# Linear attention with key-value matrices between the halves of the tokens, and splits of two heads at once, in a transformer block on one core

## The chip, the core and the metric

The kernel runs on one core of a Trainium2 chip. Its time is the device time of one execution in microseconds (us); the figure given for a kernel is the median of several runs. Every run is also described by a profile of one execution, with its own time. Engines are called as the profile calls them: PE (TensorE, matrix products; PEld are its weight loads), ACT (ScalarE), DVE (VectorE), POOL (GpSimd), SP (SyncE, which issues most DMAs).

## What is computed

One block of a transformer over 512 tokens of width 1024, in float32. The normed input is multiplied with one large matrix, and its columns are split into the inputs of two branches and their gates. The linear attention has 4 heads with keys of 128 and values of 256; the latent attention (MLA) has 8 heads, softmax over all 512 tokens, a key of 64 plain and 32 rotary features and a value of 128. Both outputs are gated, summed, projected, and followed by a squared-ReLU MLP.

The part that the change touches first is the linear attention. It is run once forwards and once backwards, and the results are added:

```python
def gla_direction(q, k, v, log_a, include_diag):
    ...
    b = jnp.cumsum(log_a, axis=3)
    q_dec = q * jnp.exp(b)
    k_dec = k * jnp.exp(-b)
    k_end = k * jnp.exp(b_last - b)
    scores = jnp.where(mask, jnp.einsum('bhnck,bhnsk->bhncs', q_dec, k_dec), 0.0)
    o_intra = jnp.einsum('bhncs,bhnsv->bhncv', scores, v)
    def step(state, inp):
        qc, kc, vc, dc = inp
        o = jnp.einsum('bhck,bhkv->bhcv', qc, state)
        state = state * dc[..., None] + jnp.einsum('bhck,bhcv->bhkv', kc, vc)
        return state, o
```

In words: a token's output is a sum over the earlier (or later) tokens of a decayed product of query and key, times the value. It can be had as scores times values, or, between two groups of tokens, by way of a matrix of keys times values (128x256) that the queries of the other group are multiplied with.

## The kernel before

**Split operands.** Most products take operands that are split into a high part of type fp32r and a low part, the rest. `mm3` (L87) makes three products of them: high x high, high x low, low x high (L88, L89, L90). `split` (L92) makes the two parts: ACT copies the high part (L93), DVE subtracts it from the source (L94). `split_scaled` (L96 to L98) does the same with a factor. A few small products take plain float32 operands, which PE works through in more than one pass; the profile counts such an instruction twice (x2).

**Linear attention.** The 512 tokens are 4 blocks of 128. For each head, class `Scaled` makes queries and keys times their decays: `near` within a block, `nxt` from a block to its neighbour in the same half of the tokens, `far` between the halves. `gla_scores` (L540) makes for each block j of keys a row of scores, in one PSUM bank (128x512): its own block (L555, and `bd` for the other direction, L543, copied under a mask by DVE, L570), its neighbour (L556) and the two blocks of the other half (L557, 256 columns). Each of the four rows is split by ACT (L571) and DVE (L566). `gla_out` (L717) multiplies: for each of 4 blocks of queries, 4 blocks of scores times 256 columns of values, `mm3` each, 48 products.

The heads stand in the loop at L1226 (heads 0 to 2), and head 3 behind it (L1273). Between a head's scores and its output PE runs a projection of 24 products (`proj_run`), and the other engines make the next head's gates: logarithms, running sums (`sums`), exponentials (`exps`, L478), `within` and `across`, whose products with broadcast factors run on POOL. In head 3 the projection is `zb5`. While it runs, ACT splits the normed latent queries (`cqhl`, L810) and makes the rotary tables (`tables`, L842: a table load, sine, cosine); DVE applies them to the rotary keys (`rotary_k`, L875: `krsin` and three more) and then makes the diagonal matrices `ckvdg` (L292) with the norms of the latent keys. Behind `gla_turn` and `gla_out` PE multiplies these with ones (`ckvrs`, L301), which spreads the norms over partitions, then runs the rotary queries (`ro`), the gates `zb6` and `zb7` and the first two heads' `uq`, `uk`, `uv`.

**Order.** In this part the order of PE, ACT, DVE and POOL is written out: `in_program_order` (L1308 to L1310) ties each instruction to the one before it in the text, for ACT and DVE from the start and for PE from the first large products up to `zb7`. SP's queue is ordered by the scheduler. All engines work strictly in the order of their queues.

**PSUM** has eight banks of 128x512, in two groups of four with the tags "at" and "mm"; a new accumulator waits until a bank of its group is released by its last reader.

**Latent attention.** `up_units` (L1007) prepares two heads at a time (a pair): it loads their weights, lets the rotary rows of the queries be copied from a shared tile by four DMAs (L1034), makes the plain rows of the queries for both heads in one accumulator (`uq`, partitions 0 to 63 the first head, 64 to 127 the second), splits each half into its own tile `q` (rows 0 to 63; the rotary rows are 64 to 95), does the same for the keys (`uk` into two of four tiles `kbuf`, whose rotary rows stay from one pair to the next), and makes the values (`uv`). Pair 0 is prepared ahead of the attention. The loop at L1330 has 32 steps n, one for each head and block of 128 queries: scores (L1064), softmax, transposes of the probabilities (L1091) and values (L1096); pair p is prepared in the steps before n = 8p, when its first head is due. In the loop the engines' orders are the scheduler's, with a few ties (`goes_behind`).

Of the kernel before, what the change touches and what calls it, by code (L numbers as in the profile page):

```python
# [13 lines left out]
I32 = mybir.dt.int32  # L14
AF = mybir.ActivationFunctionType
ALU = mybir.AluOpType
# [40 lines left out]
def tile_block(ctx: ExitStack, tc: tile.TileContext, t, out: bass.AP):  # L57
# [26 lines left out]
    def raw(x):  # L84
        return x.bitcast(F32)

    def mm3(acc, lh, ll, rh, rl, start, stop, onto=False):  # L87
        nc.tensor.matmul(acc, lh, rh, start=start, stop=False, skip_group_check=onto)  # L88
        nc.tensor.matmul(acc, lh, rl, start=False, stop=False, skip_group_check=onto)  # L89
        nc.tensor.matmul(acc, ll, rh, start=False, stop=stop, skip_group_check=onto)  # L90
# [447 lines left out]
            return self.near, self.nxt, self.far  # L538

    def gla_scores(near, nxt, far):  # L540
        bd = ps("at", "bd")
        for j in range(NT):
            nc.tensor.matmul(  # L543
                bd[:, j * P : (j + 1) * P], near["b"][:, 1, j], near["b"][:, 0, j], start=True, stop=True
            )
        bds = u2("bds")
        nc.scalar.activation(bds, bd, AF.Copy)  # L547
        res, scs = [], []
        for j in range(NT):
            sc = ps("at", f"sc{j}")  # L550
            dj = slice(j * P, (j + 1) * P)
            n = j + 1 if j % 2 == 0 else j - 1
            far_q = slice(2, 4) if j < 2 else slice(0, 2)
            far_c = slice(2 * P, 4 * P) if j < 2 else slice(0, 2 * P)
            nc.tensor.matmul(sc[:, dj], near["f"][:, 1, j], near["f"][:, 0, j], start=True, stop=True)  # L555
            nc.tensor.matmul(sc[:, n * P : (n + 1) * P], nxt[:, 1, j], nxt[:, 0, n], start=True, stop=True)  # L556
            nc.tensor.matmul(  # L557
                sc[:, far_c], far[:, 1, j], far[:, 0, far_q].rearrange("p a b -> p (a b)"),
                start=True, stop=True,
            )  # L560
            hl = u4(f"sc{j}")
            scs.append(sc)
            res.append(hl)

        def remainder(j):
            nc.vector.tensor_tensor(res[j][:, 1, :], scs[j], raw(res[j][:, 0, :]), op=ALU.subtract)  # L566

        for j, sc in enumerate(scs):
            dj = slice(j * P, (j + 1) * P)
            nc.vector.copy_predicated(sc[:, dj], after.bitcast(I32), bds[:, dj])  # L570
            nc.scalar.activation(res[j][:, 0, :], sc, AF.Copy)  # L571
            if j:
                remainder(j - 1)
        remainder(NT - 1)
        return res

# [137 lines left out]
        g = g1[i, half]  # L714
        nc.vector.scalar_tensor_tensor(g, dst, 1.0, g, op0=ALU.add, op1=ALU.mult)

    def gla_out(h, sc, rows=range(NT)):  # L717

        half, at = h // 2, (h % 2) * GDV
        accs = {j: ps("at", f"gla{h}o{j}") for j in sorted({i // 2 for i in rows})}  # L720
        c = slice(at, at + GDV)
        os = []
        for i in rows:
            o = accs[i // 2][:, (i % 2) * GDV : (i % 2 + 1) * GDV]
            tok = slice(i * P, (i + 1) * P)
            for j in range(NT):
                mm3(o, sc[j][:, 0, tok], sc[j][:, 1, tok], v[j, half][:, 0, c], v[j, half][:, 1, c],
                    j == 0, j == NT - 1)
            os.append(o)
        return os  # L730

    def gla_squares(h, os):
# [274 lines left out]
    def up_units(pr):  # L1007

        wq = stage(3, P, f"wq{pr}")
        for k in range(3):  # L1010
            nc.sync.dma_start(
                wq[:, k, :].rearrange("p (h e) -> p h e", h=2), w_uq[:, k, 2 * pr : 2 * pr + 2, 0:NOPE]
            )
        wqh, wql = halves(3, P, f"wq{pr}")
        split(wqh, wql, wq, nc.gpsimd)
        wk = stage(2, 384, f"wk{pr}")
        nc.sync.dma_start(
            wk.rearrange("p k (h e) -> p k h e", h=2), w_ukv[:, :, 2 * pr : 2 * pr + 2, :]
        )
        wh, wl = halves(2, 384, f"wk{pr}")  # L1020
        src = wk.rearrange("p k (h e) -> p k h e", h=2)
        for k in range(2):
            for c, e in ((slice(0, 128), slice(0, NOPE)), (slice(128, 384), slice(NOPE, 192))):
                split(wh[:, k, c].rearrange("p (h e) -> p h e", h=2),
                      wl[:, k, c].rearrange("p (h e) -> p h e", h=2), src[:, k, :, e], nc.gpsimd)
        if pr == 0:
            yield
        qs = []
        for i in range(2):
            q = u4(f"q{pr}{i}")  # L1030
            h = (2 * pr + i) * HALF
            for x in range(2):
                at = NOPE + x * HALF
                nc.sync.dma_start(raw(q[at : at + HALF]), raw(ro[x][h : h + HALF]))  # L1034
            qs.append(q)
        yield
        accq = up_T(wqh, wql, cq, f"uq{pr}")
        for i in range(2):
            split_scaled(qs[i][0:64, 0, :], qs[i][0:64, 1, :], accq[i * 64 : i * 64 + 64, :], QK_SCALE)
        yield  # L1040
        acck = up_T(wh[:, :, 0:128], wl[:, :, 0:128], ckv, f"uk{pr}")
        for i in range(2):
            kb = kbuf[2 * (pr % 2) + i]
            split(kb[0:64, 0, :], kb[0:64, 1, :], acck[i * 64 : i * 64 + 64, :])
        yield
        vs = []
        for j in range(2):
            acc = ps("mm", f"uv{pr}{j}")
            for i in range(2):
                tok = slice((2 * j + i) * P, (2 * j + i + 1) * P)  # L1050
                for k in range(2):
                    mm3(acc[:, i * 256 : i * 256 + 256], ckv[k][:, 0, tok], ckv[k][:, 1, tok],
                        wh[:, k, 128:384], wl[:, k, 128:384], k == 0, k == 1)
            hl = u4(f"v{pr}{j}", F32R, (P, 2, 2, 256))
            flat = [hl[:, x].rearrange("p a b -> p (a b)") for x in range(2)]
            split_scaled(*flat, acc, 0.5)
# [167 lines left out]
    rotary = Rotary()  # L1224
    pooled = traced()
    for h in range(GH - 1):  # L1226
        sc = gla_scores(*scaled_qk.parts())
        scaled_qk = Scaled(h + 1)
        gate = Gates(h + 1)
        gate.logs()  # L1230
        latent, j = ((cq_, 1), (cq_, 2), (ckv_, 0))[h]
        acc = latent.products(j)
        if h < 2:
            w_b, lows = begin_late(C_GQ + (h + 2) * P, f"gq{h + 2}")
        else:
            ckv_.begun[1], lows = begin_late(C_CKV + P, "ckv1")
        (rotary.angles, rotary.reduced, cq_.diagonals)[h]()
        gate.sums("f")
        gate.exps("f")
        lows()  # L1240
        latent.keep(j, acc)
        gate.sums("b")
        gate.exps("b")
        scaled_qk.within("f", gate.parts)
        scaled_qk.across("f", gate.parts)
        if j:
            latent.add_squares()
        if h:
            gla_turn(h - 1)
        os = gla_out(h, sc)  # L1250
        scaled_qk.within("b", gate.parts)
        rs = gla_squares(h, os)
        scaled_qk.across("b", gate.parts)
        if h < 2:
            w_k = begin_qk(h + 2, 1)
            gla_gated(h, os, rs)
            finish_qk(h + 2, 0, w_b)
            if h == 0:
                cq_.begin(2)
            else:  # L1260
                ckv_.begin(0)
                cq_.sums()
# [11 lines left out]
    sc = gla_scores(*scaled_qk.parts())  # L1274
    ckv_.sums()
    zb5 = proj_run(w_b, xT)
    cq = cq_.normed()
    cos, sin = rotary.tables()
    late = [over_rms(acc, f"b{f}") for f, acc in ((4, zb), (5, zb5))]
    rotary_k()  # L1280
# [6 lines left out]
    os = gla_out(h, sc)  # L1287
    rs = gla_squares(h, os)
    ckv_.spread()
    ckv = ckv_.normed()  # L1290
# [451 lines left out]
```

## Time and profile before

| | |
|---|---|
| runs before | 757.74, 757.77, 757.97 us; median 757.77 |
| the profiled execution | 757.43 us, of which the profile spans 755.7 |
| granted clock of PE in it | 0.999 of full speed |

| stretch, us | what runs | PE busy | DVE busy | ACT busy | POOL busy |
|---|---|---|---|---|---|
| 0 to 174.5 | first projections, large products by seven multiplications | 172.96 | 141.01 | 110.56 | 48.67 |
| 174.5 to 297.8 | linear attention, preparation of the latent attention | 123.30 | 95.51 | 79.88 | 52.40 |
| 297.8 to 377 | latent attention | 78.71 | 69.09 | 69.16 | 37.38 |
| 377 to 755 | output projection and MLP | 372.07 | 280.80 | 202.18 | 27.12 |

How to read the rows of the profile. A row of a timeline has start and duration in us, the engine, the line of the kernel, the operation, output<-inputs by name, their shapes, and how many instructions are merged in it; in brackets stands how long the engine sat idle before it and what ended that. A row of PE's waits has line and operand, who was waited for, and the us in total, the times and the longest. A row of DMA issues has the size of one and the median us from issue to landing. A matmul's duration is longer than its distance to the next, because matmuls are pipelined: the work of PE is read from the starts.

### The profile page before, as it was taken

The numbers are of one execution on the slowest core, as the hardware profiler recorded it, in microseconds if no ns is written. First come the engines' busy times: TensorE is split into PE (matmuls) and PEld (weight loads), VectorE is DVE, ScalarE is ACT, GpSimd is POOL, SyncE is SP. The second block draws the span as 40 slices with busy tenths as digits, with TensorE's granted clock in tenths as the row PEclk, the third lists the DMA queues.
The fourth block names the chain that finished last, engine by engine and source line by source line (L and its number), as shares of the span: only waits on it lengthen the run. The fifth ranks groups of instructions, "written<-read, shape, count | busy, mean of one in ns | idle before, by whom it ended". The sixth has DMA issues, their size and how long they took to land.

```text
span 755.7 us, 10257 instructions
## 1 busy us (share of the span) xinstructions
PE 747.1 (99%) x3720; PEld 632.7 (84%) x3720; DVE 586.4 (78%) x850; ACT 461.8 (61%) x780; POOL 165.6 (22%) x238
## 2 busy tenths in 40 slices
PE   9999999999999999999999999999999999999996
PEld 7888888888888888898888988888888888888885
DVE  7777886989787597898897787856696578748795
ACT  7556574686476575988865766345544555345644
POOL 0722110262662622136750100000000000000014
PEclk9999999999999999999999999999999999999999
DMA  9849582611321335228888421461126410650003
GB/s 312 259 117 240 173 175 82 113 29 29 83 55 31 49 81 119 74 84 201 260 161 262 134 57 55 141 193 57 56 63 204 123 57 2 203 158 0 29 1 111
DMA packets 94306, 87.59 MB, mean 116 GB/s; under 512 B 15696, under 2 KB 66896, under 8 KB 94256
## 3 DMA queue, kind: packets, MB, share of 16 engines
q1 hardware_dynamic: 87760, 74.33, 33.1%
q0 software_dynamic: 6208, 12.32, 9.2%
q8 instruction: 29, 0.48, 0.3%
q10 hardware_dynamic: 288, 0.28, 0.1%
q14 instruction: 21, 0.17, 0.1%
HBM read 83.25 MB, written 2.10 MB: 113 GB/s over the span
## 4 chain that ended last, share of the span: by engine, by line
PE 96%; ACT 1%; DVE 1%; issue 0%; POOL 0%; POOLq 0%; ACTq 0%
PE f L89 8%; PE f L90 8%; PE f L88 8%; PE gx L88 4%; PE gx L89 4%; PE gx L90 4%; PE first L330 3%; PE gz L89 2%; PE gz L90 2%; PE gz L88 2%; PE zb L88 1%; PE tp L1091 1%; PE zb L90 1%; PE zb L89 1%; PE wox L88 1%; PE wox L90 1%
## 5 line engine op out<-in xcount | busy, mean ns | idle before, releaser
L1681 POOL DMA_DIRECT2D gfin<-in_g_final x1 | 0.6, 628 | 283.8 <-PE f L90 283.8
L961 DVE TENSOR_TENSOR w<-w,w 128x1024 f32<-128x1024 f32 x32 | 38.7, 1220 | 0.3
L1071 DVE TENSOR_REDUCE top<-s 128x1 f32<-128x512 f32 x32 | 21.8, 681 | 3.8 <-PE s L90 3.5
L1076 ACT ACTIVATE e<-s,top 128x512 f32<-128x512 f32 x32 | 22.0, 688 | 2.9 <-DVE top L1071 2.7
L1419 DVE TENSOR_TENSOR h<-h,gx 128x512 f32<-128x512 f32 x32 | 21.5, 681 | 1.9 <-PE gx L90 1.8
L94 DVE TENSOR_TENSOR pT<-tp,pT 128x512 fp32r<-128x512 f32 x32 | 21.7, 681 | 1.5 <-ACT pT L93 1.3
L93 ACT ACTIVATE pT<-tp 128x512 fp32r<-128x512 f32 x32 | 19.0, 596 | 2.2 <-PE tp L1091 2.1
L1091 PE MATMUL tp<-ident,e 128*128 128x128 f32 x128 | 19.5, 274 | 0.3 <-ACT e L1082 0.2
L88 PE MATMUL av<-pT,v 128*128 128x256 f32 x64 | 19.1, 298 | 0.0
L93 ACT ACTIVATE ghb<-y 128x512 fp32r<-128x512 f32 x16 | 10.1, 632 | 14.0 <-DVE y L907 14.0
L1485 ACT ACTIVATE fa<-f 128x512 f32<-128x512 f32 x32 | 18.5, 578 | 0.0
L1091 PEld LDWEIGHTS tp<-ident,e 128*128 128x128 f32 x128 | 15.1, 140 | 4.0 <-ACT e L1082 1.0
L89 PE MATMUL av<-pT,v 128*128 128x256 f32 x64 | 18.2, 285 | 0.0
L90 PE MATMUL av<-pT,v 128*128 128x256 f32 x64 | 18.2, 284 | 0.0
L547 ACT ACTIVATE bds<-bd 128x512 f32<-128x512 f32 x4 | 2.4, 598 | 20.9 <-PE bd L543 20.9
L93 ACT ACTIVATE b_00h<-w 128x1024 fp32r<-128x1024 f32 x7 | 7.4, 1059 | 12.6 <-PE gz L90 6.0
L93 ACT ACTIVATE b_20h<-w 128x1024 fp32r<-128x1024 f32 x7 | 7.4, 1061 | 12.1 <-PE gx L90 6.0
L93 ACT ACTIVATE b_10h<-w 128x1024 fp32r<-128x1024 f32 x7 | 7.4, 1060 | 12.1 <-PE gx L90 6.0
L88 PE MATMUL s<-kbuf,q 96*128 96x512 f32 x32 | 14.2, 443 | 0.2 <-ACT e L1076 0.2
L1494 ACT ACTIVATE px<-fa 128x256 f32<-128x256 f32 x32 | 13.4, 418 | 1.0
L957 POOL DMA_DIRECT2D w<-in_w_out x10 | 12.3, 1403 | 7.6 <-DVE bo60l L94 6.5
L636 POOL DMA_DIRECT2D gvw<-in_w_in x4 | 4.8, 1227 | 38.7 <-DVE gvw L641 34.0
(1731 smaller groups left out, 2947.6 us busy)
## 6 DMA issues: line engine op xcount, KB each, us to landing
w<-in_w_ff SPq DMA_DIRECT2D x64, 256.0 KB, 3.4
w<-in_w_out POOLq DMA_DIRECT2D x10, 512.0 KB, 9.3
grw<-in_w_in SPq DMA_DIRECT2D x8, 512.0 KB, 9.0
zaw<-in_w_in SPq DMA_DIRECT2D x8, 512.0 KB, 7.0
gvw<-in_w_in SPq DMA_DIRECT2D x8, 512.0 KB, 4.5
w<-in_w_out SPq DMA_DIRECT2D x16, 256.0 KB, 6.2
x<-in_xt SPq DMA_DIRECT2D x8, 256.0 KB, 5.3
vw<-in_w_first SPq DMA_DIRECT2D x8, 256.0 KB, 5.5
```

The costliest lines, as they stand in the source:

```text
L88: nc.tensor.matmul(acc, lh, rh, start=start, stop=False, skip_group_check=onto)
L89: nc.tensor.matmul(acc, lh, rl, start=False, stop=False, skip_group_check=onto)
L90: nc.tensor.matmul(acc, ll, rh, start=False, stop=stop, skip_group_check=onto)
L93: nc.scalar.activation(hi, src, AF.Copy)
L94: rest.tensor_tensor(lo, src, raw(hi), op=ALU.subtract)
L330: nc.tensor.matmul(f_accs[i], a[:, i * P : (i + 1) * P], b, start=k == 0 and x == 0, stop=k == KD - 1 and x == 2)
L961: nc.vector.tensor_tensor(wq[dst][g], wq[x][g], wq[y][g], op=op)
L1071: nc.vector.tensor_reduce(top, acc, axis=AX.X, op=ALU.max, negate=True)
L1076: nc.scalar.activation(e, acc, AF.Exp, bias=top, accum_out=tot[:, qt % 2 : qt % 2 + 1])
L1091: nc.tensor.transpose(tp[:, k * P : (k + 1) * P], e[:, k * P : (k + 1) * P], ident)
L1419: nc.vector.tensor_tensor(hc, hc, acc, op=op)
L1485: nc.scalar.activation(a, acc, AF.Relu)
```

## The change

It has two parts.

**Linear attention.** The score rows shrink to the blocks within a half: two banks (`sc0`, `sc1`) with 2x2 blocks each, in place of four rows. PE transposes the four blocks of `far` keys into a bank `kt` (tokens on partitions), which ACT and DVE split (`keys`). A new function `gla_state` multiplies these with the values, 12 products, into one matrix of 128x256 for each half of the tokens; ACT copies them into SBUF (`state`). In `gla_out` each block of queries takes 2 blocks of scores (24 products for the head), and then one float32 product of its `far` queries with the other half's matrix. `gla_state` stands behind the projection and the running sums in the loop, ahead of `gate.exps("f")`; in head 3 it stands behind `cq_.normed()` and ahead of `rotary.tables()`.

**Splits of two heads.** For the pairs 1 and 2 (heads 2 to 5), the accumulators of queries and keys are split as a whole, 128 partitions at once, into the first head's tile. A DMA then copies rows 64 to 127 to rows 0 to 63 of the second head's tile. The first head's rotary rows of the queries, which the split writes over, are copied in behind that by two DMAs; the rotary rows of the first key tile are restored from the second by another. Pairs 0 and 3 stay as they are.

```diff
     def gla_scores(near, nxt, far):
...
+        scs = [ps("at", f"sc{g}") for g in range(2)]
+        def block(j, i):
+            at = (j % 2) * 256 + (i % 2) * P
+            return scs[j // 2][:, at : at + P]
+        for j in range(NT):
+            n = j + 1 if j % 2 == 0 else j - 1
+            nc.tensor.matmul(block(j, j), near["f"][:, 1, j], near["f"][:, 0, j], start=True, stop=True)
+            nc.tensor.matmul(block(j, n), nxt[:, 1, j], nxt[:, 0, n], start=True, stop=True)
+        kt = ps("at", "kt")
+        for j in range(NT):
+            nc.tensor.transpose(kt[:, j * P : (j + 1) * P], far[:, 1, j], ident)
         bds = u2("bds")
         nc.scalar.activation(bds, bd, AF.Copy)
+        res = [u4(f"sc{g}") for g in range(2)]
+        for g in range(2):
+            for j in (2 * g, 2 * g + 1):
+                nc.vector.copy_predicated(block(j, j), after.bitcast(I32), bds[:, j * P : (j + 1) * P])
+            nc.scalar.activation(res[g][:, 0, :], scs[g], AF.Copy)
+        for g in range(2):
+            nc.vector.tensor_tensor(res[g][:, 1, :], scs[g], raw(res[g][:, 0, :]), op=ALU.subtract)
+        keys = u4("kT")
+        split(keys[:, 0, :], keys[:, 1, :], kt)
+        return res, keys, far
+
+    def gla_state(h, keys):
+        half, at = h // 2, (h % 2) * GDV
+        c = slice(at, at + GDV)
+        acc = ps("at", f"gla{h}st")
         for j in range(NT):
...
+            tok = slice(j * P, (j + 1) * P)
+            mm3(acc[:, (j // 2) * GDV : (j // 2 + 1) * GDV], keys[:, 0, tok], keys[:, 1, tok],
+                v[j, half][:, 0, c], v[j, half][:, 1, c], j % 2 == 0, j % 2 == 1)
+        state = u2(f"gla{h}s")
+        nc.scalar.activation(state, acc, AF.Copy)
+        return state
...
-    def gla_out(h, sc, rows=range(NT)):
+    def gla_out(h, sc, state, far):
...
+        for i, o in enumerate(os):
+            g = i // 2
+            for x in range(2):
+                j = 2 * g + x
+                tok = slice(x * 256 + (i % 2) * P, x * 256 + (i % 2 + 1) * P)
+                mm3(o, sc[g][:, 0, tok], sc[g][:, 1, tok], v[j, half][:, 0, c], v[j, half][:, 1, c],
+                    i % 2 == 0 and x == 0, False, True)
+        for i, o in enumerate(os):
+            other = 1 - i // 2
+            nc.tensor.matmul(
+                o, far[:, 0, i], state[:, other * GDV : (other + 1) * GDV], start=False, stop=True,
+                skip_group_check=True,
+            )
...
+        apart = pr in (0, MH // 2 - 1)
+        qs = [u4(f"q{pr}{i}") for i in range(2)]
+        for i in range(2):
+            if apart or i == 1:
+                rotary_rows(i)
         yield
         accq = up_T(wqh, wql, cq, f"uq{pr}")
...
+            split_scaled(qs[0][:, 0, :], qs[0][:, 1, :], accq, QK_SCALE)
+            nc.sync.dma_start(raw(qs[1][0:64]), raw(qs[0][64:128]))
+            rotary_rows(0)
         yield
         acck = up_T(wh[:, :, 0:128], wl[:, :, 0:128], ckv, f"uk{pr}")
...
+            split(kbs[0][:, 0, :], kbs[0][:, 1, :], acck)
+            nc.sync.dma_start(raw(kbs[1][0:64]), raw(kbs[0][64:128]))
+            nc.sync.dma_start(raw(kbs[0][64:96]), raw(kbs[1][64:96]))
...
     for h in range(GH - 1):
-        sc = gla_scores(*scaled_qk.parts())
+        sc, keys, far = gla_scores(*scaled_qk.parts())
...
         gate.sums("f")
+        state = gla_state(h, keys)
         gate.exps("f")
...
     h = GH - 1
...
     cq = cq_.normed()
+    state = gla_state(h, keys)
     cos, sin = rotary.tables()
```

More of the change, by code (lines that the diff above doesn't have):

```diff
@@ L546, in gla_scores @@
         bds = u2("bds")
         nc.scalar.activation(bds, bd, AF.Copy)
-        res, scs = [], []
-        for j in range(NT):
[L550 to L575, printed above, removed]
+        res = [u4(f"sc{g}") for g in range(2)]
@@ L715, in za_rows @@
         nc.vector.scalar_tensor_tensor(g, dst, 1.0, g, op0=ALU.add, op1=ALU.mult)
-    def gla_out(h, sc, rows=range(NT)):
+    def gla_out(h, sc, state, far):
         half, at = h // 2, (h % 2) * GDV
-        accs = {j: ps("at", f"gla{h}o{j}") for j in sorted({i // 2 for i in rows})}
+        accs = [ps("at", f"gla{h}o{g}") for g in range(2)]
         c = slice(at, at + GDV)
[L722 to L729, printed above, removed]
+        os = [accs[i // 2][:, (i % 2) * GDV : (i % 2 + 1) * GDV] for i in range(NT)]
+        for i, o in enumerate(os):
[11 more added lines that the diff above has]
+            )
         return os
@@ L1027, in up_units, with rotary_rows @@
             yield
-        qs = []
-        for i in range(2):
-            q = u4(f"q{pr}{i}")
+        def rotary_rows(i):
             h = (2 * pr + i) * HALF
@@ L1033, in up_units @@
                 at = NOPE + x * HALF
-                nc.sync.dma_start(raw(q[at : at + HALF]), raw(ro[x][h : h + HALF]))
-            qs.append(q)
+                nc.sync.dma_start(raw(qs[i][at : at + HALF]), raw(ro[x][h : h + HALF]))
+        apart = pr in (0, MH // 2 - 1)
[3 more added lines that the diff above has]
+                rotary_rows(i)
         yield
         accq = up_T(wqh, wql, cq, f"uq{pr}")
-        for i in range(2):
-            split_scaled(qs[i][0:64, 0, :], qs[i][0:64, 1, :], accq[i * 64 : i * 64 + 64, :], QK_SCALE)
+        if apart:
+            for i in range(2):
+                split_scaled(qs[i][0:64, 0, :], qs[i][0:64, 1, :], accq[i * 64 : i * 64 + 64, :], QK_SCALE)
+        else:
+            split_scaled(qs[0][:, 0, :], qs[0][:, 1, :], accq, QK_SCALE)
+            nc.sync.dma_start(raw(qs[1][0:64]), raw(qs[0][64:128]))
+            rotary_rows(0)
         yield
         acck = up_T(wh[:, :, 0:128], wl[:, :, 0:128], ckv, f"uk{pr}")
-        for i in range(2):
-            kb = kbuf[2 * (pr % 2) + i]
-            split(kb[0:64, 0, :], kb[0:64, 1, :], acck[i * 64 : i * 64 + 64, :])
+        kbs = kbuf[2 * (pr % 2) : 2 * (pr % 2) + 2]
+        if apart:
+            for i, kb in enumerate(kbs):
+                split(kb[0:64, 0, :], kb[0:64, 1, :], acck[i * 64 : i * 64 + 64, :])
+        else:
+            split(kbs[0][:, 0, :], kbs[0][:, 1, :], acck)
+            nc.sync.dma_start(raw(kbs[1][0:64]), raw(kbs[0][64:128]))
+            nc.sync.dma_start(raw(kbs[0][64:96]), raw(kbs[1][64:96]))
         yield
@@ L1249, in tile_block @@
             gla_turn(h - 1)
-        os = gla_out(h, sc)
+        os = gla_out(h, sc, state, far)
         scaled_qk.within("b", gate.parts)
@@ L1273, in tile_block @@
     h = GH - 1
-    sc = gla_scores(*scaled_qk.parts())
+    sc, keys, far = gla_scores(*scaled_qk.parts())
     ckv_.sums()
@@ L1286, in tile_block @@
     gla_turn(h - 1)
-    os = gla_out(h, sc)
+    os = gla_out(h, sc, state, far)
     rs = gla_squares(h, os)
```

## The prediction

> **What bounds the kernel now.** I read the page first (busy shares, the chain that ended last), then PE's waits, then the timelines of PE, ScalarE and VectorE around the change.
>
> ```profile
> span 755.7 us, 10257 instructions
> PE 747.1 (99%) x3720; PEld 632.7 (84%) x3720; DVE 586.4 (78%) x850; ACT 461.8 (61%) x780; POOL 165.6 (22%) x238
> ...
> PE 96%; ACT 1%; DVE 1%; issue 0%; POOL 0%; POOLq 0%; ACTq 0%
> ```
>
> ```profile
> PE warm L320 <- POOL ident masks.py:199: 1.5, 1, 1.5
> PE tp L1091 <- ACT e L1082: 0.2, 1, 0.2
> PE s L88 <- ACT e L1076: 0.2, 1, 0.2
> ```
>
> TensorE is busy from end to end. Its three named waits come to 1.9 us, of which 1.5 is the start. So a matmul that goes shortens the run by its full pitch (start to start), a matmul that comes lengthens it likewise, and a new wait of PE costs its whole length. The other engines matter only where they make PE late. The busy time of a group is no price, since matmuls overlap; I take pitches.
>
> **The linear attention, one head.** Head 0 on PE, scores and then output:
>
> ```profile
> 174.55 1.05 PE L543 MATMUL bd<-qkb 128*128 128x128 f32 x8
> 175.44 0.39 PE L555 MATMUL sc<-qkf 128*128 128x128 f32 x2
> 175.66 0.39 PE L556 MATMUL sc<-qk 128*128 128x128 f32 x2
> 175.89 0.60 PE L557 MATMUL sc<-qk 128*128 128x256 f32 x2
> 176.32 0.38 PE L555 MATMUL sc<-qkf 128*128 128x128 f32 x2
> ...
> 179.19 0.40 PE L451 MATMUL gateb<-z,gate_b 128*128 128x512 f32 x1
> ...
> 184.86 0.28 PE L88 MATMUL gla0o<-gv,sc 128*128 128x256 f32 x1
> ...
> 190.62 0.40 PE L88 MATMUL gq<-xT,gq2h 128*128 128x512 f32 x1
> ```
>
> The trace before has transposes of the form that is added (four of 128x128 into one bank), in the attention; first their group on the page, then four of them with what follows:
>
> ```profile
> L1091 PE MATMUL tp<-ident,e 128*128 128x128 f32 x128 | 19.5, 274 | 0.3 <-ACT e L1082 0.2
> ```
>
> ```profile
> 327.71 0.60 PE L1091 MATMUL tp<-ident,e 128*128 128x128 f32 x4
> 328.07 0.47 PE L88 MATMUL s<-kbuf,q 96*128 96x512 f32 x1
> 328.38 0.40 PE L89 MATMUL s<-kbuf,q 96*128 96x512 f32 x1
> 328.62 0.40 PE L90 MATMUL s<-kbuf,q 96*128 96x512 f32 x1
> ```
>
> Prices: a float32 product of 128 columns 0.22 us (175.44 to 175.66), of 256 columns 0.43 (175.89 to 176.32), a product of 256 columns from split operands 0.12 (48 of them from 184.86 to 190.62). Four transposes hold PE 0.36 us, and the product behind them takes 0.31 where the next takes 0.24: 0.44 together.
>
> 1. Scores. Before, bd to gate b takes 4.64 us (174.55 to 179.19). After: bd 0.89, eight products of 128 columns 1.78, four transposes with their tail 0.44, gate f 0.23, together 3.34: **-1.30**. The four far products (1.72) are gone, the transposes have come.
> 2. Key-value matrices. New: 4 blocks x 3 products = 12 x 0.12 = **+1.44**.
> 3. Output. Before, 48 products, 184.86 to 190.62, 5.76 us. After: 24 x 0.12 = 2.88, and four float32 products of 256 columns with the state, of the very form of L557, 4 x 0.43 = 1.72; together 4.60: **-1.16**.
>
> Net -1.02 us a head: half the output products go, and half of that returns as key-value products. Four heads: -4.1 us, if PE waits for nothing.
>
> ScalarE and VectorE in the scores: four score copies become two plus the keys' split, and VectorE loses one subtraction; the keys have the time of a projection, 24 products of 512 columns at 0.23 or 5.5 us, to get ready before PE asks. New on ScalarE is the state's copy, 0.6 us (an activation of this shape, the sine below, takes 0.63). It waits for the last key-value product, and everything later on ScalarE stands behind it, since ScalarE's and VectorE's order here is that of the program. In heads 0 to 2 that is the reload of the exponential table and the exponentials. They then start about when they do now on the head's own clock, while PE is 1 us ahead. On VectorE a second scan and a difference (L468, L473) still stand before their first use, and they hide it: I cost it at nothing; uncovered, it would be that 1 us per head.
>
> **Head 3 is different.** There the sine table stands behind the copy:
>
> ```profile
> 265.79 1.83 ACT L810 ACTIVATE cqhl<-cqc 128x512 fp32r<-128x512 f32 x3 [1.62 <-DVE cqc L808]
> 267.63 1.28 ACT L844 ACT_TABLE_LOAD   x1
> 268.93 0.63 ACT L844 ACTIVATE sin<-ang 128x512 f32<-128x512 f32 x1
> ```
>
> ```profile
> 270.36 0.48 DVE L878 TENSOR_SCALAR krsin<-sin,gvec 32x512 f32<-32x512 f32 x1
> ...
> 273.39 0.68 DVE L292 TENSOR_TENSOR ckvdg<-ident,ckvrh 128x512 fp32r<-128x512 f32 x1
> 273.99 0.68 DVE L292 TENSOR_TENSOR ckvdg<-ident,ckvrl 128x512 fp32r<-128x512 f32 x1
> ```
>
> ```profile
> 269.20 0.39 PE L90 MATMUL zb<-xT,zb5l 128*128 128x512 f32 x1
> 269.44 0.38 PE L756 MATMUL y<-ident,grb 128*128 128x128 f32 x2
> ...
> 270.23 0.36 PE L88 MATMUL gla3o<-gv,sc 128*128 128x256 f32 x1
> ...
> 276.06 0.62 PE L301 MATMUL ckvrs<-ckvdg,ones_r 128*128 128x512 f32 x2
> 276.52 0.39 PE L88 MATMUL ro<-cqhl,wr0h 128*128 128x512 f32 x1
> ```
>
> Before, ScalarE loads the table and makes the sine while PE still runs zb5. VectorE goes from krsin without a break to the diagonals ckvdg, done at 274.67, and PE spreads them at 276.06: 1.6 us to spare for the second product. After, counted on this clock with head 3's own shift alone: zb5 ends 1.30 earlier, 268.14; key-value products until 269.58, the last done about 269.74; copy 269.79 to 270.39; table load to 271.67; sine 271.69 to 272.32; krsin 272.37, **2.0 us later than now**. The diagonals are done at 276.68. PE is there earlier than now: 269.58 + 0.79 (turn) + 2.96 + 1.72 = 275.05. It waits until 276.73 for the second product, and L301's successor starts at 276.96 instead of 275.51: a new wait of **+1.45**, more than head 3 saves.
>
> The delay of VectorE runs on through rotary_q to the split that frees the PSUM bank of zb7's accumulator:
>
> ```profile
> 290.45 0.69 DVE L98 SCALAR_TENSOR_TENSOR q<-uq,q 64x512 fp32r<-64x512 f32 x1 [0.66 <-ACT q L97]
> ...
> 292.33 0.40 PE L88 MATMUL zb<-xT,zb7h 128*128 128x512 f32 x1
> ```
>
> Now 1.2 us to spare (291.14 to 292.33). After: bank free at about 293.1, PE there at 292.33 + 0.44 = 292.77: **+0.35**. Then the 24 products of zb7 (5.5 us) let VectorE and ScalarE catch up.
>
> **The splits of two heads.** For two pairs of heads, four ScalarE and four VectorE instructions over 64 partitions become two and two over 128; both last 0.6 to 0.7 us whatever the partitions. No PE work changes. PE is late once near them:
>
> ```profile
> 312.55 0.28 PE L90 MATMUL av<-pT,v 128*128 128x256 f32 x1
> 312.98 0.50 PE L88 MATMUL s<-kbuf,q 96*128 96x512 f32 x1 [0.15 <-ACT e L1076]
> ```
>
> So the gain lies between 0 and 0.43 - 0.12 = 0.31 us; I take 0, since a new order of the instructions of ScalarE and VectorE could cost as much. New are DMAs from SBUF to SBUF on SP's queue: query halves (256 KB), then head 2's rotary rows, which before were sent long ahead; key halves (256 KB), then 128 KB to restore the rotary rows of the key. For head 2 they must land before its first scores:
>
> ```profile
> 304.30 0.67 DVE L98 SCALAR_TENSOR_TENSOR q<-uq,q 64x512 fp32r<-64x512 f32 x1
> ...
> 306.67 0.68 DVE L94 TENSOR_TENSOR kbuf<-uk,kbuf 64x512 fp32r<-64x512 f32 x1
> ...
> 315.16 0.40 PE L88 MATMUL s<-kbuf,q 96*128 96x512 f32 x1
> ```
>
> ```profile
> q<-ro SPq DMA_DIRECT2D x16, 64.0 KB, 2.5
> ...
> bo11f<-in_w_out SPq DMA_DIRECT2D x2, 256.0 KB, 3.1
> ...
> kbuf<-kbuf SPq DMA_DIRECT2D x3, 128.0 KB, 3.9
> ```
>
> 256 KB between SBUF rows is not in the trace: at least 2.5 us, and 6.7 if the 1.4 us between the 64 and 128 KB rows is paid per 64 KB. I take 3.5, near the 256 KB row, because the 3.9 were three at once. Keys split 307.35, copied 310.9, rows restored (3.9) 314.8: before 315.16, cost 0. The loads of w_out behind them on SP's queue wait too; they are for products late in the attention, and that is their cover. Head 4's chain is the same with a whole head more of attention work beside it.
>
> **Sum.** 3 x -1.02, then head 3: -1.02 + 1.45 + 0.35 = +0.78; together **-2.3 us**. The profiled execution took 757.43 us (span 755.7 and 1.7 around it): 755.1. The median shown, 757.77, is 0.34 above it: I predict **755.5**.
>
> [...] The transposes' rows give a pitch near 0.1 us. [...]
>
> **Rivals.**
>
> - *No new wait in head 3.* The sum is -4.1: 753.7. For it: PE shows almost no wait anywhere, and 1.6 us were spare. Against: the order of ScalarE is the program's. It needs the diagonals 1.45 us earlier than I count. Chance 0.18.
> - *Head 2 waits a little.* SP sends in order; if the rotary rows stand ahead of the key copy, that copy starts only when the queries have landed: 305.0 + 3.5 + 1.2 (two issues) + 3.5 + 3.9 = 317.1, a wait of 1.9: 757.4, no change. Chance 0.20.
> - *Slower: the same place at the high DMA price.* 305.0 + 6.7 + 1.2 + 6.7 + 3.9 = 323.5, a wait of 8.3: 763.8. With copies of x us the chain ends at 310.1 + 2x; it turns the result slower by over 0.2% from a wait of 3.8, x = 4.45. For it: the 128 KB row is slow. Against: 256 KB from HBM land in 3.1. Chance 0.13.
> - *Transposes are paid at their duration*: 4 x 0.274 = 1.10 instead of 0.44, +2.6 over four heads: 758.1. Against it: the pitch above. Chance 0.03. [...]
>
> **Numbers.** Forecast 0.46, its own range 754.4 to 756.6 (pitches to 0.02, the two waits to half their size). 0.2% is 1.5 us, about what a measurement of this kernel can tell from no change. Faster by more (below 756.25): nearly all of the forecast, 0.43, and the first rival, 0.18: 0.61. Same: the rest of the forecast, the second and the last rival: 0.26. Slower: 0.13. The range takes in the first and second rivals and the last: 753.2 to 758.3.
>
> **What would show it.** PE from bd to gate b 3.3 us a head; 36 split products and four float32 products of 256 columns behind each; a PE wait before L301's successor (ckvrs) of about 1.4 us released by VectorE, with ScalarE idle before the state's copy of head 3; a shorter PE wait at zb7; no wait of PE before head 2's first scores. I am wrong if ckvrs starts without a wait, if the correction products have another pitch than 0.43, if a head's scores wait on GpSimd's far blocks, or if the attention from first scores to last takes more than 0.5 us longer or shorter.

## The result, and the profile after

The kernel after the change takes **755.15 us** (median of 8 runs, 754.4 to 755.97), the kernel before 757.2 (757.04 to 757.97): ratio **0.9972**, 95% interval 0.9963 to 0.998. The forecast was 755.5, range 753.2 to 758.3. The profiled execution took 754.4 us.

From the page of the kernel after, and its waits of PE:

```profile
span 752.7 us, 10206 instructions
...
PE 742.9 (99%) x3688; PEld 628.0 (83%) x3688; DVE 580.5 (77%) x842; ACT 457.7 (61%) x776; POOL 165.7 (22%) x238
```

```profile
PE warm L320 <- POOL ident masks.py:199: 1.5, 1, 1.5
PE ckvrs L301 <- DVE ckvdg L292: 1.0, 1, 1.0
PE zb L88 <- DVE q L98: 0.5, 1, 0.5
```

PE is still the bound. The two short waits for ACT in the latent attention are gone, and two new ones have come, both in head 3 and both at the places that the prediction named.

PE's timeline in head 0, scores, key-value matrices and output:

```profile
173.93 1.05 PE L545 MATMUL bd<-qkb 128*128 128x128 f32 x8
174.81 0.39 PE L556 MATMUL sc<-qkf 128*128 128x128 f32 x2
...
176.60 0.60 PE L560 MATMUL kt<-ident,qk 128*128 128x128 f32 x4
176.96 0.48 PE L451 MATMUL gatef<-z,gate_f 128*128 128x512 f32 x1
177.27 0.40 PE L451 MATMUL gateb<-z,gate_b 128*128 128x512 f32 x1
...
182.98 0.28 PE L88 MATMUL gla0st<-gv,kT 128*128 128x256 f32 x1
...
184.41 0.28 PE L88 MATMUL gla0o<-gv,sc 128*128 128x256 f32 x1
...
187.30 1.89 PE L742 MATMUL gla0o<-gla0s,qk 128*128 128x256 f32 x8
188.84 0.58 PE L88 MATMUL gq<-xT,gq2h 128*128 128x512 f32 x1
189.25 0.39 PE L89 MATMUL gq<-xT,gq2h 128*128 128x512 f32 x1
```

Read from the starts: bd to gate b 3.34 us, the key-value products 1.43, the output 184.41 to 188.84, 4.43, and 0.41 instead of 0.23 for the first product behind it, 4.61 together.

Where the time went, by stage. Each number is the distance of two starts on PE in one profiled execution: from `bd` of a head to `bd` of the next, in head 3 to the first latent scores, then from the first to the 32nd scores.

| stage, us | before | after | linear part alone | splits alone | tables ahead |
|---|---|---|---|---|---|
| head 0 | 26.98 | 26.02 | 26.03 | 26.97 | 26.02 |
| head 1 | 28.80 | 27.84 | 27.84 | 28.81 | 27.84 |
| head 2 | 28.30 | 27.34 | 27.34 | 28.30 | 27.34 |
| head 3: bd to `ro` (past `ckvrs`) | 17.89 | 18.45 | 18.44 | 17.89 | 16.84 |
| head 3: `ro` to first scores | 21.28 | 22.04 | 21.76 | 21.27 | 21.29 |
| latent attention, scores 1 to 32 | 73.77 | 72.78 | 73.81 | 72.76 | 72.79 |

After against before: 3 x -0.96, head 3 +1.32, latent attention -0.99, sum **-2.55 us**. What lies behind (377.3 us from the last scores on) is the same to 0.1. The two profiled spans differ by 3.0 us; 0.62 of it lies ahead of head 0, in instructions that the change leaves alone, which took 174.55 us before, 173.93 after and 174.71 in experiment 10. The medians differ by 2.05.

Head 3, which is slower. ACT, then DVE, then PE of the kernel after:

```profile
261.55 1.83 ACT L826 ACTIVATE cqhl<-cqc 128x512 fp32r<-128x512 f32 x3 [1.73 <-DVE cqc L824]
266.29 0.60 ACT L584 ACTIVATE gla3s<-gla3st 128x512 f32<-128x512 f32 x1 [2.92 <-PE gla3st L90]
266.91 1.28 ACT L860 ACT_TABLE_LOAD   x1
268.20 0.63 ACT L860 ACTIVATE sin<-ang 128x512 f32<-128x512 f32 x1
```

```profile
264.43 1.28 DVE L375 TENSOR_TENSOR zb<-zb,R 128x512 f32<-128x512 f32 x2
268.87 0.48 DVE L894 TENSOR_SCALAR krsin<-sin,gvec 32x512 f32<-32x512 f32 x1 [3.15 <-ACT sin L860]
...
272.50 0.68 DVE L292 TENSOR_TENSOR ckvdg<-ident,ckvrl 128x512 fp32r<-128x512 f32 x1
```

```profile
269.78 1.89 PE L742 MATMUL gla3o<-gla3s,qk 128*128 128x256 f32 x8
272.63 1.10 PE L301 MATMUL ckvrs<-ckvdg,ones_r 128*128 128x512 f32 x2 [0.97 <-DVE ckvdg L292]
273.58 0.40 PE L88 MATMUL ro<-cqhl,wr0h 128*128 128x512 f32 x1
...
290.07 0.47 PE L88 MATMUL zb<-xT,zb7h 128*128 128x512 f32 x1 [0.48 <-DVE q L98]
```

ACT sits idle for 2.92 us ahead of the state's copy, with the table load queued behind it; DVE then idles 3.15 us for the sine, and PE 0.97 for DVE's diagonals. The second product of L301 waits once more: 0.95 us from L301 to `ro`, where it was 0.46. One copy in an in-order queue has cost three engines a wait each.

SP's queue for heads 2 and 3 (second pair), and PE at head 2's first scores:

```profile
302.82 0.52 SPq L1064 DMA_DIRECT2D q<-q  x1
304.36 0.50 SPq L1074 DMA_DIRECT2D kbuf<-kbuf  x1
306.05 1.18 SPq L1048 DMA_DIRECT2D q<-ro  x2
307.33 0.53 SPq L1075 DMA_DIRECT2D kbuf<-kbuf  x1
```

```profile
313.15 0.40 PE L88 MATMUL s<-kbuf,q 96*128 96x512 f32 x1
```

The scheduler put the key copy ahead of the rotary rows. The query copy landed in 3.1 us, the key copy in 2.9, the restored rotary rows in 2.3, at 309.7: 3.5 us before PE asks, and PE doesn't wait.

### The profile page after: what moved, and what is told of

The parts are those of the page before. It is cut to its first block, busy times and chain, and to the rows that moved or that the text cites. A ratio compares the mean times of both kernels' runs of the same rounds, so it can differ in the third digit from the quotient of the medians.

```text
span 752.7 us, 10206 instructions
## 1 busy us (share of the span) xinstructions
PE 742.9 (99%) x3688; PEld 628.0 (83%) x3688; DVE 580.5 (77%) x842; ACT 457.7 (61%) x776; POOL 165.7 (22%) x238
## 4 chain that ended last, share of the span: by engine, by line
PE 95%; DVE 2%; ACT 1%; issue 1%; POOL 0%; POOLq 0%; ACTq 0%
PE f L88 8%; PE f L89 8%; PE f L90 8%; PE gx L88 4%; PE gx L90 4%; PE gx L89 4%; PE first L330 3%; PE tp L1122 2%; PE gz L88 2%; PE gz L90 2%; PE gz L89 2%; PE zb L88 1%; PE zb L89 1%; PE zb L90 1%; PE av L88 1%; PE s L88 1%
```

## The experiments

Theories ahead of the first runs. **T**: the heads give about 1 us each; head 3 loses it because the state's copy stands ahead of the sine table on ACT; the splits give 1 us of their own in the latent attention. Rival **R**: the splits give nothing, the latent attention's gain comes with the linear part, and the wait in head 3 isn't due to the place of the copy.

**1. The linear part alone.**

```diff
-        apart = pr in (0, MH // 2 - 1)
+        apart = True
```

> The linear attention as in the change, the splits of two heads as before. Theory (T): three heads gain 0.96 us each, head 3 loses 1.3 us by its two new waits, the latent attention is as before: 1.6 us faster than before, ratio 0.9979. Rival (R): the 1 us that the latent attention gained in the changed kernel is not the splits' doing but comes from when and in which order it begins, so this kernel has it too: 2.6 us faster, 0.9966, with s31 72.8 us behind s0 instead of 73.8.

Measured: 755.95 us, ratio 0.9979 [0.9971, 0.9988]. Its latent attention takes 73.81 us, as before the change (table above).

**2. The splits alone**: the kernel before with the new `up_units`.

> The kernel before with the splits of two heads for pairs 1 and 2 and nothing else. T: 1.0 us faster than before (0.9987), the last scores 72.8 us behind the first where before it is 73.8, no wait of PE before the scores of heads 2 and 4. R: no difference, 1.0000. If SP's copies come late, slower.

Measured: 756.57, ratio 0.9991 [0.9982, 0.9999]; latent attention 72.76. R falls in its first half: the latent attention's gain is the splits'. Each part keeps to its stage, with one exception: from `ro` to the first scores the kernel after takes 0.28 us more than the linear part alone (22.04 against 21.76). That is one subtraction on DVE, here in the kernel after and then in the linear part alone:

```profile
280.19 0.97 DVE L885 TENSOR_TENSOR roa<-roa,rob 128x512 f32<-128x512 f32 x1
```

```profile
280.40 0.69 DVE L885 TENSOR_TENSOR roa<-roa,rob 128x512 f32<-128x512 f32 x1
```

It took 0.69 us before the change too. Why it varies, no run shows.

**3. Tables ahead of the state**, in head 3:

```diff
     cq = cq_.normed()
-    state = gla_state(h, keys)
     cos, sin = rotary.tables()
+    state = gla_state(h, keys)
```

> The changed kernel, in head 3 alone the rotary tables made ahead of the state's copy on ScalarE (two lines of the program change places; PE's order stays). T: the waits of PE at ckvrs (1.6 us) and at the bank of zb7 (0.5) are the table and the sine held up behind the copy, and both go: 2.1 us below the changed kernel, ratio to before 0.9945. R: PE waits there because it now comes earlier to a VectorE chain that could not be faster: the same time as the changed kernel, 0.9972.

Measured: **752.72 us**, ratio 0.9938 [0.9926, 0.9951], faster than both kernels. ACT's timeline, and all of PE's waits:

```profile
264.16 1.28 ACT L860 ACT_TABLE_LOAD   x1
265.45 0.63 ACT L860 ACTIVATE sin<-ang 128x512 f32<-128x512 f32 x1
...
267.06 0.60 ACT L584 ACTIVATE gla3s<-gla3st 128x512 f32<-128x512 f32 x1 [0.35 <-PE gla3st L90]
```

```profile
PE warm L320 <- POOL ident masks.py:199: 1.5, 1, 1.5
```

ACT does the tables in the time in which it waited for PE, and is done with them 0.35 us before the last key-value product lets it copy the state. The copy ends at 267.66, 2.9 us ahead of the products that need it (270.54). Both new waits are gone: head 3 takes 38.13 us, 1.04 less than before the change, as the other heads do. PE's order is the same in both kernels. So the waits come from the place of one instruction on ACT, R falls in its second half, and together they cost 40.49 - 38.13 = 2.36 us.

**4. The state's copy of head 3 on DVE**, which leaves ACT free by another way:

```diff
-        nc.scalar.activation(state, acc, AF.Copy)
+        if h < GH - 1:
+            nc.scalar.activation(state, acc, AF.Copy)
+        else:
+            nc.vector.tensor_copy(state, acc)
```

> The changed kernel, the state's copy of head 3 made by VectorE instead of ScalarE, at the same place of the program. T: the sine is no longer held, VectorE waits some 0.5 us for the last key-value product and copies in 0.7; krsin starts 1.9 us earlier than in the changed kernel; the wait at ckvrs goes, a wait of 0.2 to 0.4 at the bank of zb7 stays: 1.8 us below the changed kernel, 0.9949. R: as the changed kernel, 0.9972, or later, since VectorE has the copy on top.

Measured: 753.98, ratio 0.9959 [0.9945, 0.9972]: the right direction, but less than I expected. DVE's timeline shows why:

```profile
266.66 0.69 DVE L587 COPY gla3s<-gla3st 128x512 f32<-128x512 f32 x1 [1.72 <-PE gla3st L90]
267.27 1.28 DVE L375 TENSOR_TENSOR zb<-zb,R 128x512 f32<-128x512 f32 x2
268.58 0.48 DVE L897 TENSOR_SCALAR krsin<-sin,gvec 32x512 f32<-32x512 f32 x1
```

The copy now makes DVE wait 1.72 us for PE, and holds up the two products with the gate (L375, 1.28 us), which in the kernel after ran during DVE's own wait for the sine. `krsin` starts 13.03 us behind head 3's `bd`; it is 11.73 before, 13.74 after, 10.62 with the tables ahead. PE still waits 0.3 us at L301 and 0.3 us at zb7. The wait moved to the other in-order queue.

All that follow start from the kernel of experiment 3 (752.72 us).

**5. The seventh and eighth head split together too**, `apart = pr == 0`.

> The kernel with the tables ahead of the state (752.72 us), and beside it the splits of two heads at once for the seventh and eighth head too: three of four pairs. Theory (the splits together pay by the ScalarE and VectorE time that they take off a stretch in which those engines lag behind TensorE): the third such pair gives at most what one of the two did, 0 to 0.3 us more, so 752.4 to 752.7, ratio 0.9934 to 0.9938, first to last latent scores 72.5 to 72.8. Rival (the three transfers of the key chain, up to 5.6 us for 256 KB and 5.4 for 128 KB beside loads, land after the fourth pair's first scores product is due): TensorE shows a wait of 0.5 to 2 us behind a DMA ahead of that product, time 753.2 to 754.7, ratio 0.9945 to 0.9965.

Measured: **757.86** (12 runs, 755.03 to 760.12), ratio 1.0005 [0.9991, 1.0018]: the rival, and worse than it said. SP's queue, PE, and PE's granted clock in stretches (the columns are: stretch, its length, PE busy with matmuls, PEclk, the DMA engines' busy share, GB/s):

```profile
339.73 0.50 SPq L1064 DMA_DIRECT2D q<-q  x1
342.23 0.50 SPq L1074 DMA_DIRECT2D kbuf<-kbuf  x1
346.88 1.36 SPq L1048 DMA_DIRECT2D q<-ro  x2
348.35 0.54 SPq L1075 DMA_DIRECT2D kbuf<-kbuf  x1
```

```profile
355.89 0.47 PE L88 MATMUL s<-kbuf,q 96*128 96x512 f32 x1 [2.92 <-DMA kbuf<-kbuf]
```

```profile
350.00:352.00 2.00, 2.00 (x17) 1.00 1.31 180
356.00:358.00 2.00, 2.00 (x8) 0.60 1.01 361
358.00:360.00 2.00, 2.00 (x9) 0.55 0.97 264
360.00:362.00 2.00, 2.00 (x16) 1.00 1.09 254
```

Here the copies run beside the loads of `w_out` (DMA share about 1). SP waits 4.0 us for the query copy ahead of the rotary rows, and the restored rows of the key, 128 KB, need 7.4 us. PE waits 2.92 us (3.20 from start to start), and then runs about four microseconds at a granted clock whose means over 2 us are 0.60 and 0.55: products of 512 columns that lie 0.23 apart elsewhere lie 0.43 apart. From the 24th to the 27th scores that makes 4.8 us more than in experiment 3, of which only 3.1 is the step with the wait.

**6. All four pairs together**, `apart = False`.

> The kernel with the tables ahead of the state (752.72 us), with the splits of two heads at once for all four pairs, the first too. This puts the price on the slow chain of transfers that was the rival on the slower side. Theory: in the first pair the keys are multiplied at about 288 and the first scores product is due at about 294; split 0.6, copy 3 to 5, rotary keys 2.3 to 5 make 294 to 299, so TensorE waits 0.5 to 4 us ahead of the first latent scores (5.5 us from the last zb product there to the first scores becomes 6 to 9.5), total 753 to 756.5, ratio 0.9945 to 0.999. Rival (the chain is short enough at any place): no wait there, and two splits fewer ahead of it give 0 to 0.3 us, total 752.2 to 752.7, ratio 0.9932 to 0.9938.

Measured: 761.73, ratio 1.0058 [1.0042, 1.0073]. I had the place wrong: the first pair's chain lands at 293.3 and PE has its first scores at 293.49, without a wait. The loss is at the fourth pair again:

```profile
PE s L88 <- DMA kbuf<-kbuf: 6.5, 1, 6.5
```

There SP waits 9.1 us for one query copy of 256 KB, and behind PE's wait the granted clock is 0.50 from 359 to 363 us and 0.72 from 363 to 365.

**7 and 8. Which engine's time do the splits save?** The second copy on ACT, or the second subtraction on DVE, is issued again for queries and keys of heads 2 to 5, and overwritten by the DMA:

```diff
+            nc.scalar.activation(qs[1][0:64, 0, :], accq[64:128, :], AF.Copy, scale=QK_SCALE)
             nc.sync.dma_start(raw(qs[1][0:64]), raw(qs[0][64:128]))
```

> The kernel with the tables ahead of the state (752.72 us); for the third to sixth head the second ScalarE copy of queries and of keys that the change removed (64 x 512, 0.6 us each, four in all) is issued again, its values then overwritten by the transfer, so nothing else changes. Theory (the 1.0 us that the splits together gave is ScalarE time): most of it goes, first to last latent scores 73.3 to 73.8 where it was 72.8, total 753.2 to 753.7, ratio 0.9945 to 0.9952. Rival (it is VectorE time, or the order of the transfers): 72.8 and 752.7, ratio 0.9938.

> The kernel with the tables ahead of the state (752.72 us); for the third to sixth head the second VectorE subtraction of queries and of keys that the change removed (64 x 512, 0.68 us each, four in all) is issued again, its values then overwritten by the transfer. Theory (ScalarE time is what the splits gave): first to last latent scores stay at 72.8 to 73.0, total 752.7 to 752.9, ratio 0.9938 to 0.994. Rival (VectorE time is what they gave): 73.3 to 73.8, total 753.2 to 753.7, ratio 0.9945 to 0.9952.

Measured: with ACT's 753.54, 0.9948 [0.9936, 0.996], latent attention 73.01; with DVE's 752.81, 0.9941 [0.9929, 0.9953], latent attention 72.79. ACT's four copies cost 0.22 us, less than I expected, DVE's nothing. So with either set put back most of the 1.0 stays: 0.77 with ACT's, 0.98 with DVE's. But both kernels also have PE's products in another order than experiment 3, because the scheduler orders the latent attention anew for each program; so these two runs don't settle it.

**9 to 11. Instructions or order?** With the splits together the scheduler had put 75 products of PE in another place. These runs take splits and order apart: the base with the splits head by head, and two kernels in which PE's order in the latent attention is tied to that of the other version.

```diff
+    products = [i for i in nc.cur_bb.bb.instructions if i.engine == mybir.EngineType.PE and "Matmul" in type(i).__name__]
+    pinned = [products[at + x] for at, count in pinned for x in range(count)]
+    for this, following in zip(pinned, pinned[1:]):
+        issued_after(following, this.name)
```

> The kernel with the tables ahead of the state (752.72 us), but with all splits head by head as before the change: the base for the two runs beside it. First to last latent scores 73.8 as in the linear part alone, so 752.72 + 1.0 = 753.7 us, ratio 0.9951. (If the new order in the fourth head had moved the latent part too: 72.8, 752.7, ratio 0.9938.)

> Tables ahead of the state, all splits head by head as before the change, but TensorE's products in the latent attention tied into the order that the scheduler gave them with the splits together (75 of them stand elsewhere than with the splits apart). Theory I (the 1.0 us is what the removed ScalarE and VectorE instructions took): it isn't regained by the order alone, first to last latent scores 73.6 to 74.3, total 753.5 to 754.2, ratio 0.9949 to 0.9958, with waits of TensorE for ScalarE. Theory O (the 1.0 us is the other order of the products): 72.8 to 73.0, total 752.7 to 752.9, ratio 0.9938 to 0.9941.

> Tables ahead of the state, splits of two heads at once for the third to sixth head, but TensorE's products in the latent attention tied into the order that the scheduler gave them with the splits apart. Theory I (the removed instructions): the gain stays, first to last latent scores 72.8 to 73.1, total 752.7 to 753.0, ratio 0.9938 to 0.9942. Theory O (the order): the gain is gone, 73.6 to 73.8, total 753.5 to 753.7, ratio 0.9949 to 0.9952. Half in both runs would mean that both have a part.

Measured: 753.21, 0.9942 [0.993, 0.9955]; 755.23, 0.9972 [0.996, 0.9983]; 753.56, 0.9951 [0.9937, 0.9964]. The first has its latent attention as forecast (73.78 us). By these totals the second run fits neither theory, and the third, with 73.66 us for the latent attention, lies where theory O put it. But they mix several losses, so I read them by step. The starts of the first and the 30th scores on PE, splits apart in the old order, then splits together in the old order:

```profile
293.30 0.40 PE L88 MATMUL s<-kbuf,q 96*128 96x512 f32 x1
...
361.99 0.48 PE L88 MATMUL s<-kbuf,q 96*128 96x512 f32 x1
```

```profile
293.45 0.40 PE L88 MATMUL s<-kbuf,q 96*128 96x512 f32 x1
...
360.55 0.48 PE L88 MATMUL s<-kbuf,q 96*128 96x512 f32 x1
```

| first to 30th scores, us | old order of PE | new order of PE |
|---|---|---|
| splits apart | 68.69 | 69.18 |
| splits together | 67.10 | 67.71 |

The same products lie between these starts in all four. The splits are worth 1.59 us in the old order and 1.47 in the new, and the new order costs 0.49 and 0.61. That settles the sign: the gain isn't PE's new order, which gives back about a third of it.

The traces also show where it is won. With the splits apart PE waits for ACT's `e`; here the longest such wait in front of the 30th scores, in the old order and then in the new:

```profile
355.00 0.66 PE L1122 MATMUL tp<-ident,e 128*128 128x128 f32 x4 [0.23 <-ACT e L1113]
```

```profile
310.01 0.50 PE L88 MATMUL s<-kbuf,q 96*128 96x512 f32 x1 [1.21 <-ACT e L1107]
```

In the old order the splits together gain 0.41 us around the 8th scores, 0.45 ahead of the 27th and 0.30 ahead of the 29th, where PE with the splits apart sits idle for 0.14, 0.23 and 0.12 us (for the 0.14 and the 0.12 the profile names nobody). In the new order the wait ahead of the 8th scores makes 1.34 of the 1.47. With the splits together none of this idle time is there. What the ties don't hold is the order of ACT and DVE, which the scheduler makes anew as well and which differs between the rows of the table. That the removed instructions, and not this order, end the waits is argued, not shown.

Behind the 30th scores both tied kernels lose 1.5 us: there PE waits for ACT's `e` (1.26 us in splits together, old order), which the untied kernels don't show. The kernel with splits apart in the new order loses 0.79 us ahead of the first scores too. These losses are why the totals mislead.

**12. The old order only where the splits changed it**, free behind:

> As new_splits_old_order, but TensorE's products are tied into the old order only in the stretch in which the splits changed it (200 products around the second and third pair), and free behind it. There 28 of the 31 steps took 0.6 us less than with the scheduler's own order, and 1.26 us was lost in one wait of a transpose for ScalarE two steps before the end. Theory (that wait comes from the ties behind the changed stretch): it is gone, first to last latent scores 72.1 to 72.4, total 752.0 to 752.4, ratio 0.9929 to 0.9934, below the 752.7 of the best so far. Rival (it comes from where ScalarE's instructions stand once the stretch before is shorter): the wait stays, 73.4 to 73.7, total 753.3 to 753.6, ratio 0.9946 to 0.9951.

Measured: 752.88, 0.9946 [0.9932, 0.9959]. The latent attention takes 72.30 us, as the theory had it, so the 1.26 us wait did come from the ties. The total doesn't get better, though: from the last scores to the MLP's first product it is 48.09 us instead of 47.30, and PE's waits have a new row:

```profile
PE av L88 <- DVE tb L1150: 0.9, 1, 0.9
```

So what was won ahead of it is lost to a wait for DVE. Why it comes stays open: the kernels of experiments 5 and 6, in which PE gets there later, have the same row, and in all three the scheduler has put DVE's instructions in another order than in experiment 3. That kernel stays the best version.

## Why the prediction was right, step by step

- *Scores -1.30, key-value matrices +1.44, output -1.16.* Measured in head 0: 3.34 - 4.64 = -1.30, +1.43, 4.61 - 5.76 = -1.15. The head as a whole gains 0.96 instead of 1.02; the 0.06 I did not trace. The pitch was the right price: four transposes of 128x128 and their tail took 0.67 - 0.23 = 0.44 us (176.60 to 177.27, less one product's pitch). The rival that paid them at their mean duration, 4 x 0.274 = 1.10, is not borne out by this trace.
- *State copy at nothing in heads 0 to 2.* Right: no wait of PE there, and the three heads gain alike.
- *Head 3: a new wait at L301, and a second one at zb7's bank.* Both are there, released by the named instructions, and `krsin` is 2.01 us later on the head's clock, as counted (2.0). The waits are bigger than I made them: 1.61 instead of 1.45 to `ro` (18.45 against 16.84 with the tables ahead), and 0.75 instead of 0.35 behind it (22.04 against 21.29). Of the 0.75, 0.28 is DVE's longer subtraction of experiment 2, whose cause is open; without it the term is 0.47. Head 3 lost 1.32, forecast 0.78.
- *Splits: "the gain lies between 0 and 0.31 us; I take 0".* This is the term that was mis-sized: -0.99 us. The prediction's own sign of being wrong, the attention shorter by more than 0.5 us, has come true here. I looked for PE's waits only near the changed instructions and took the largest as the upper end. I had shown the other wait for ACT, `PE tp L1091 <- ACT e L1082: 0.2`, and left it out, though it stands ahead of the 27th scores, where the splits together gain 0.45 us in the old order. ACT and DVE have little slack in the latent attention: each is busy for 69 of its 79.2 us, and more around the changed instructions. Before the change, with the columns stretch, length, and busy time of PE, PEld, DVE, ACT and POOL:

```profile
312.00:324.00 12.00, 11.85 (x72) 10.08 (x71) 11.11 (x21) 11.54 (x27) 3.53 (x6) 1.00 0.42 116
```

  DVE is busy for 11.11 of 12 us and ACT for 11.54. What is saved counts many steps later: in the same order of products the lead of the splits together grows to 0.55 us by the 13th scores, 0.81 by the 19th and 1.60 by the 29th. The new order, which I set against the gain, costs 0.5 to 0.6, not all of it.
- *DMA chain of head 2.* Right in its result (no wait), too dear in its terms: the copies took 3.1 and 2.9 us for 3.5, the restored rows 2.3 for 3.9. The slower rival's high DMA price is real, but at the fourth pair, which the change leaves alone, and not at head 2 (experiments 5 and 6; the two copies of 256 KB took 10.5 and 10.8 us in experiment 6). There the restored rows, and not the key copy, stand behind SP's wait for the query copy.
- *Sum -2.3.* The stages give -2.55, the medians -2.05. The errors of head 3 (+0.54) and of the heads (+0.18) and that of the splits (-0.99) partly cancel, which is luck: the forecast was nearer than its terms. It also stood on 757.77, the median of three runs before; that of eight is 757.2, which would have made it 754.9.

## What to carry to other kernels

Before you put a copy that waits for the bound engine on an in-order queue, look at what stands behind it: moving two lines so that work which needs nothing from that engine goes first was worth more (2.4 us) than the change itself. When an engine beside the bound is busy for nearly nine tenths of its time (ACT and DVE here for 69 of 79.2 us), price an instruction taken off it over the whole stretch, not by the one wait that stands next to it, and hold the bound engine's order when you test it. Copies through DMAs that land in 3 us and cost nothing in one stretch took 10.5 and 10.8 us beside weight loads and made PE wait 6.5 us (experiment 6), so place such a chain by the DMA share of its stretch.

## What the runs showed of the hardware

- A DMA of 256 KB from SBUF to SBUF landed in 2.9 and 3.1 us where the DMA engines were half busy (share 0.51 from 302 to 308 us after the change), in 4.4 and 5.6 at the next pair (0.60 from 322 to 329 us), and needed up to 10.8 beside the loads of `w_out` (experiment 6, 1.06 from 339 to 349 us); the 128 KB of restored rows took 2.3 us at head 2 after the change and 7.4 at the fourth pair in experiment 5.
- Behind a wait of 2.92 us (experiment 5) PE's granted clock had means of 0.60 and 0.55 over the next two stretches of 2 us and 1.00 over the one after them, and 1.7 us were lost beyond the 3.1 of the step with the wait. Behind a wait of 6.5 us (experiment 6) it was 0.50 from 359 to 363 us, 0.72 from 363 to 365 and 1.00 from 365 to 367. Behind the waits of 0.97 us (head 3 after the change) and 1.26 us (experiment 11) products of 512 columns lay 0.23 us apart, as elsewhere.
- Instructions ahead of head 0 that no edit touches took 173.93 us after the change, 174.55 before and 174.71 in experiment 10, so these spans differ by up to 0.78 us with no cause in the change; most distances within a stage agree to 0.03 us (head 0: 26.98 and 26.97 in the two kernels with the old linear part, 26.02, 26.03 and 26.02 in the three with the new). The exception found is DVE's subtraction at L885, 0.69 to 0.97 us, which moved a stage by 0.28.
